# A Hyena/S5 diffusion step on one core: one taller, wider product in the filter stage, and the point-wise work of the long convolutions on VectorE alone

## The chip, the cores and the metric

The kernel runs on 1 core of one Trainium2 chip. The metric is the device time of one execution in microseconds (us). The engines are TensorE (PE; its weight loads are shown as PEld), VectorE (DVE), ScalarE (ACT), GpSimd (POOL) and SyncE (SP, which issues most transfers).

## The reference, cut to what matters

Two groups of tokens (1,024 latent, 256 context) run through a Hyena layer, an S5 layer and a feed-forward block behind each. The change lies in the Hyena layer: in the making of its filters and in its two long convolutions.

```python
def _hyena_filter_spectrum(L, w1, b1, w2, b2, w3, freq):
    ...
    h = jnp.sin(fr * (z @ w1.astype(f32) + b1.astype(f32)))
    h = jnp.sin(fr * (h @ w2.astype(f32) + b2.astype(f32)))
    h = (h @ w3.astype(f32)).reshape(L, HY_ORDER, 2, D_MODEL)
    ...
    h = h * decay[:, None, None, :]
    h = h / (jnp.sum(jnp.abs(h), axis=(0, 2), keepdims=True) + EPS)
    ...
    return jnp.fft.rfft(k, axis=0)

def _fft_longconv(v, k_f, bias):
    L = v.shape[1]
    vf = v.astype(jnp.float32)
    v_f = jnp.fft.rfft(vf, n=2 * L, axis=1)
    y = jnp.fft.irfft(v_f * k_f[None], n=2 * L, axis=1)[:, :L]
    return y + vf * bias.astype(jnp.float32)

def _hyena_mixer(u, j, p):
    ...
    v = _fft_longconv(v, k_f[:, 0], fb[0]) * x1.astype(jnp.float32)
    v = _fft_longconv(v, k_f[:, 1], fb[1]) * x2.astype(jnp.float32)
    ...
```

## The kernel before, in words

Stages follow one another on the one core: `filters` (the filters and their spectra, written to memory), `hyena_in` (input projection and short convolution, with the S5 tables beside it), `hyena_core` (the two long convolutions), `hyena_out`, a feed-forward block, the S5 scan, the gated projection and the second feed-forward block. The code only gives each engine's work; with `schedule_with_timeline_sim=True` a scheduler interleaves the steps, and each engine then runs its own list in that order.

**Products in three terms.** Where fp32 accuracy is wanted, both operands are split into a high and a low part in the format fp32r, and `mm3` (lines 35 to 38) issues hi·hi, hi·lo and lo·hi.

**`filters`, `gen` (line 415).** There are 8 units: 4 blocks `db` of 256 channels times 2 orders `o`. For each unit `gen` runs over 5 pairs `pr` of 128-row time tiles, with both directions `d` (forward and backward) of the filter. `w3s` holds the high part of the weights in partitions 0 to 63 and their low part in partitions 64 to 127. `h2h` holds the high part of the 64 hidden values twice, so one product over 128 partitions gives hi·(hi+lo) (line 424). `h2l` holds the low part once, in 64 partitions; the second product (line 425) contracts those 64 with the high part of the weights alone. Each direction has 256 columns and its own pair of products, so a time tile takes four matmuls, by turns over 128 and over 64 partitions. The DVE multiplies the result by the decay (line 426). POOL then adds and subtracts the directions (`sd`, lines 463 and 464) and sums absolute values (line 437), ACT and DVE split the result (line 467), PE transforms it (`odd`, `even`, `ctxs`), DVE combines (lines 512 to 517) and SP stores the spectrum. Beside it run the modulation products (`ada_stream`, lines 270 and 280) and the reading of x (`x_stream`).

**`hyena_core`.** 24 units: 8 groups (order, block), in each two latent halves `kt` and one context unit. `fwd` (line 753) is the forward transform on PE, from which ACT writes `E`. `point` (line 776) multiplies by the spectrum `K`: 15 point-wise steps for a latent unit and 7 for a context unit, with `AB` as scratch, each over 2 to 8 planes of 256 columns. `CUT = 168` splits every step: columns 0 to 167 go to DVE, 168 to 255 to POOL, as one instruction on each (line 813). `inverse` (line 851) is the inverse transform on PE, in fp32; in the trace each of its matmuls is two records. `evac` multiplies by the gate on DVE (line 886), `split_v` splits the result (line 226) for the second convolution. `E` has 5 buffers, `AB` and `K` two each.

Of the kernel before, what the change touches and what calls it, by code (L numbers as in the profile page):

```python
# [7 lines left out]
F32 = mybir.dt.float32  # L8
F32R = mybir.dt.float32r
# [299 lines left out]

LATW, M3W, CTXW = 4096, 1024, 512  # L310
TT = 10
CUT = 168


def load_f(K, io, fp, step=LATW + CTXW):
# [22 lines left out]
def filters(K, io):  # L338

    nc, tc = K.nc, K.tc  # L340
    V, P = nc.vector, nc.gpsimd
    ADD, SUB, MUL = ALU.add, ALU.subtract, ALU.mult
    with ExitStack() as c:
# [2 lines left out]
        hp = c.enter_context(tc.tile_pool(name="fhd", bufs=1, reuse_waits="tile"))  # L346
        cp = c.enter_context(tc.tile_pool(name="fc", bufs=1, reuse_waits="tile"))
        h2h = cp.tile([128, 1280], F32R, name="h2h")
        h2l = cp.tile([64, 1280], F32R, name="h2l")
        m3 = [cp.tile([128, M3W], F32R, name=f"m3{i}") for i in range(2)]  # L350
        W3, DEC, HD, ACC, SD, FB = {}, {}, {}, {}, {}, {}

# [14 lines left out]
        with ExitStack() as c2:  # L367
# [21 lines left out]
            for lhs, rhs, M, dst, bc in ((w1, zT, 64, a1, 0), (w2, a1, 128, a2, 1)):  # L389
                o = 0  # L390
                for n in TB:
                    ps = K.psum.tile([128, 512], F32, tag="ps", name="ps")
                    nc.tensor.matmul(ps[:M, :n], lhs, rhs[:, o:o + n], start=True, stop=True)
                    d, s = dst[:, o:o + n], t[:M, o:o + n]
                    nc.scalar.activation(out=d, in_=ps[:M, :n], func=AF.Identity, scale=bf[:M, 2:3], bias=bias[:M, bc:bc + 1])
                    reduce_2pi(K, V, d, s)
                    nc.scalar.activation(out=d, in_=d, func=AF.Sin)
                    if bc:
                        nc.scalar.copy(h2h[:, o:o + n], d)
                        V.tensor_tensor(out=h2l[:, o:o + n], in0=d[0:64], in1=h2h[0:64, o:o + n].bitcast(F32), op=SUB)  # L400
                    o += n
                    for _ in range(2 * bc):
                        next(adas)
# [11 lines left out]
        def gen(u, pr):  # L415
# [3 lines left out]
            for i in range(2):  # L419
                tt = pr * 2 + i  # L420
                ps = K.psum.tile([128, 2, 256], F32, tag="ps", name="ps")
                for d in range(2):
                    q = o * 2 + d
                    nc.tensor.matmul(ps[:, d], h2h[:, tt * 128:(tt + 1) * 128], w[:, q], start=True, stop=False)
                    nc.tensor.matmul(ps[:, d], h2l[:, tt * 128:(tt + 1) * 128], w[0:64, q], start=False, stop=True)
                V.tensor_tensor(out=hd[:, i], in0=ps, in1=dec[:, i:i + 1, :].to_broadcast([128, 2, 256]), op=MUL)
            HD[u, pr] = hd
            if o and db < 3:
# [307 lines left out]
def hyena_core(K, io):  # L736
    nc, tc = K.nc, K.tc
    with ExitStack() as c:
# [6 lines left out]
        G = gp.tile([128, LATW + CTXW], F32, name="G")  # L745
        ep = c.enter_context(tc.tile_pool(name="e", bufs=5, reuse_waits="tile"))
        ADD, SUB, MUL = ALU.add, ALU.subtract, ALU.mult
        parts = [(nc.vector, slice(0, CUT)), (nc.gpsimd, slice(CUT, 256))]

        def pl(pool, tag, n):  # L750
            return pool.tile([128, n // 256, 256], F32, tag=tag, name=tag)
# [24 lines left out]
        def point(E, Kt, ctx):  # L776

            R = 2 if ctx else 4
            AB = pl(ap, "AB", 512 * R)
            v4 = lambda t: t.rearrange("p (o a) n -> p o a n", a=2)  # L780
            todo = []
            for eng, sl in parts:
                e, w, k = (t[:, :, sl] for t in (E, AB, Kt))
                er = e.rearrange("p (a r) n -> p a r n", a=2)
                x = e
                if ctx:
                    ops = [(x[:, 2:4], x[:, 2:4], x[:, 0:2], SUB)]
                else:
                    ac = er[:, :, 2:4]
                    bd = w[:, 4:8].rearrange("p (a r) n -> p a r n", a=2)  # L790
                    ops = [(bd, er[:, :, 0:2], ac, SUB),
                           (x[:, 0:2], ac[:, :, 0], ac[:, :, 1], ADD),
                           (x[:, 4:6], ac[:, :, 0], ac[:, :, 1], SUB),
                           (x[:, 2:8:5], bd[:, :, 0], bd[:, ::-1, 1], ADD),
                           (x[:, 6:2:-3], bd[:, :, 0], bd[:, ::-1, 1], SUB)]
                ops += [(v4(w), v4(x), v4(k)[:, :, ::-1, :], MUL),
                        (x, x, k, MUL),
                        (v4(x)[:, :, 0], v4(x)[:, :, 0], v4(x)[:, :, 1], SUB),
                        (v4(x)[:, :, 1], v4(w)[:, :, 0], v4(w)[:, :, 1], ADD)]
                if ctx:  # L800
                    ops += [(w[:, 0:2], x[:, 0:2], x[:, 2:4], ADD),
                            (w[:, 2:4], x[:, 0:2], x[:, 2:4], SUB)]
                else:
                    ops += [(w[:, 0:4], x[:, 0:4], x[:, 4:8], ADD),
                            (w[:, 4:8], x[:, 0:4], x[:, 4:8], SUB),
                            (x[:, 0:2], w[:, 0:2], w[:, 2:4], ADD),
                            (x[:, 4:6], w[:, 0:2], w[:, 2:4], SUB),
                            (x[:, 6:2:-3], w[:, 4:6], w[:, 7:5:-1], ADD),
                            (x[:, 2:8:5], w[:, 4:6], w[:, 7:5:-1], SUB)]
                todo.append((eng, ops))  # L810
            for eng, ops in todo:
                for out, x, y, f_ in ops:
                    eng.tensor_tensor(out=out, in0=x, in1=y, op=f_)  # L813
            return AB if ctx else E

        order = [(0, 0), (0, 1), (1, 0), (0, 2), (1, 1), (0, 3), (1, 2), (1, 3)]
# [918 lines left out]
```

## Time and profile before

| | us |
|---|---|
| time, median of 3 runs (lowest to highest) | 3817.84 (3814.34 to 3820.59) |
| the profiled execution, its own time | 3819.98 |
| its span in the trace | 3818.1 |
| PE / DVE / POOL / ACT busy | 3440.9 / 2473.1 / 1218.6 / 964.8 |

The profile cuts the span into 40 slices of some 95 us. A digit is the busy share of an engine in that slice, in tenths; the row PEclk is the TensorE clock that was granted, in tenths of full speed. A share of the whole span is an average over stages with different limits, so the stages are read apart: `filters` lies at about 20 to 490 us of the span, `hyena_in` at 470 to 875, `hyena_core` at 875 to 1,270, and everything behind it at 1,270 to 3,818. A matmul's duration holds the draining of the array, so what one matmul costs in a row of them is the distance from its start to the next start.

### The profile page before, as it was taken

How to read it: one execution, taken by the hardware profiler on the slowest of the kernel's cores; microseconds unless marked ns; L12 is line 12 of the kernel's file. 1: busy time of each engine (PE TensorE's matmuls, PEld its weight loads, DVE VectorE, ACT ScalarE, POOL GpSimd, SP SyncE). 2: the span in 40 equal slices, each digit the busy share in tenths (PEclk: the TensorE clock that was granted, in tenths of full speed). 3: DMA queues.
4: the chain of work that ended last, by engine and by line, in shares of the span. 5: the costliest groups of instructions: out<-in, count | busy, mean ns of one | idle time of the engine just before them, and what ended most of it. 6: DMA issues, size and time to landing. Idle time of an engine off the chain costs nothing.

```text
span 3818.1 us, 48757 instructions
## 1 busy us (share of the span) xinstructions
PE 3440.9 (90%) x19238; PEld 2913.7 (76%) x19238; DVE 2473.1 (65%) x3846; ACT 964.8 (25%) x1674; POOL 1218.6 (32%) x1062
## 2 busy tenths in 40 slices
PE   6999979997777799999999998556999999999997
PEld 4777758886666588888888886555887888888886
DVE  5766798768999656655566445997236445445545
ACT  3343443332121342111111113123224111111112
POOL 3555520008999533443344001662112000000002
PEclk9777889998888899999999998777999999999998
DMA  7554545345433611222212112564101111110101
GB/s 219 175 176 155 172 153 155 121 178 190 142 116 103 201 60 60 73 69 66 67 62 70 45 39 84 137 169 133 45 28 45 34 39 39 39 39 34 45 28 56
DMA packets 292444, 368.27 MB, mean 96 GB/s; under 512 B 38415, under 2 KB 230615, under 8 KB 283256
## 3 DMA queue, kind: packets, MB, share of 16 engines
q1 hardware_dynamic: 278392, 343.53, 28.0%
q10 hardware_dynamic: 11520, 11.15, 1.3%
q0 software_dynamic: 2304, 10.49, 0.8%
q8 instruction: 152, 2.49, 0.3%
q14 instruction: 76, 0.62, 0.1%
HBM read 268.49 MB, written 91.29 MB: 94 GB/s over the span
## 4 chain that ended last, share of the span: by engine, by line
PE 55%; DVE 9%; DMA 1%; issue 1%; POOL 1%; ACT 1%; ACTq 0%; SPq 0%; DVEq 0%; POOLq 0%
PE ps L36 18%; PE ps L37 18%; PE ps L38 18%; DVE Z L1382 2%; DVE Z L1383 1%; DVE E L813 1%; DVE nw L89 1%; DVE x L1492 0%; DVE h L1334 0%; DMA yr<-yv 0%; DVE x L184 0%; DVE R L1392 0%; PE ps L1230 0%; DVE R L1391 0%; DVE AB L813 0%
## 5 line engine op out<-in xcount | busy, mean ns | idle before, releaser
L36 PE MATMUL ps<-hh,hi 128*128 128x512 f32 (+1 forms) x2688 | 953.0, 358 | 19.3 <-ACT hh L225 16.1
L37 PE MATMUL ps<-hl,hi 128*128 128x512 f32 (+1 forms) x2688 | 957.9, 357 | 8.9 <-POOL hl L96 5.8
L38 PE MATMUL ps<-hh,lo 128*128 128x512 f32 (+1 forms) x2688 | 953.2, 355 | 0.0
L184 DVE SCALAR_TENSOR_TENSOR x<-ps,mod,x 128x512 f32<-128x512 f32 (+1 forms) x1056 | 629.9, 653 | 11.3 <-PE ps L38 11.3
L36 PEld LDWEIGHTS ps<-hh,hi 128*128 128x128 f32 x2688 | 507.4, 189 | 99.9 <-ACT hh L225 17.6
L37 PEld LDWEIGHTS ps<-hl,hi 128*128 128x128 f32 x2688 | 508.6, 189 | 88.6 <-POOL hl L96 11.7
L167 DVE TENSOR_TENSOR nw<-nw,ps 128x512 f32<-128x512 f32 x132 | 78.8, 597 | 766.6 <-PE ps L38 760.8
L38 PEld LDWEIGHTS ps<-hh,lo 128*128 128x128 f32 x2688 | 507.4, 189 | 73.3 <-issue 0.5
L57 POOL TENSOR_TENSOR st<-st,sq 128x512 f32<-128x512 f32 (+1 forms) x72 | 91.7, 1277 | 1179.0 <-ACT sq L56 1176.6
L37 PE MATMUL ps<-gl,hi 128*128 128x512 f32 (+1 forms) x1056 | 375.3, 355 | 0.0
L36 PE MATMUL ps<-gh,hi 128*128 128x512 f32 (+1 forms) x1056 | 373.4, 355 | 1.2 <-DVE x L184 1.2
L38 PE MATMUL ps<-gh,lo 128*128 128x512 f32 (+1 forms) x1056 | 374.2, 354 | 0.0
L32 DVE TENSOR_TENSOR lo<-raw,hi 128x1024 fp32r<-128x1024 f32 x156 | 208.0, 1335 | 96.5 <-ACT hi L31 96.4
L31 ACT CAST hi<-raw 128x1024 fp32r<-128x1024 f32 x156 | 163.3, 1049 | 350.2 <-PE ps L37 318.1
L36 PEld LDWEIGHTS ps<-gh,hi 128*128 128x128 f32 x1056 | 198.8, 188 | 32.1 <-DVE x L184 2.1
L37 PEld LDWEIGHTS ps<-gl,hi 128*128 128x128 f32 x1056 | 199.0, 188 | 29.4 <-issue 1.2
L38 PEld LDWEIGHTS ps<-gh,lo 128*128 128x128 f32 x1056 | 199.0, 188 | 28.8 <-issue 0.7
L36 PE MATMUL ps<-hh,wh 128*128 128x512 f32 (+1 forms) x576 | 210.3, 366 | 9.8 <-ACT hh L95 9.8
L37 PE MATMUL ps<-hl,wh 128*128 128x512 f32 (+1 forms) x576 | 208.9, 363 | 7.7 <-DVE hl L92 7.4
L38 PE MATMUL ps<-hh,wl 128*128 128x512 f32 (+1 forms) x576 | 207.6, 361 | 1.8 <-POOL wl L226 1.8
L170 ACT CAST gh<-nw 128x512 fp32r<-128x512 f32 x132 | 72.2, 547 | 483.7 <-DVE nw L167 483.7
L166 ACT ACTIVATE nw<-ps 128x512 f32<-128x512 f32 x132 | 69.3, 525 | 490.9 <-PE ps L38 489.9
(369 smaller groups left out, 6153.3 us busy)
## 6 DMA issues: line engine op xcount, KB each, us to landing
adaw<-in_ada_w SPq DMA_DIRECT2D x96, 512.0 KB, 5.1
raw<-in_w13p SPq DMA_DIRECT2D x88, 512.0 KB, 3.6
raw<-in_w2p SPq DMA_DIRECT2D x44, 512.0 KB, 3.5
kspec<-KO SPq DMA_DIRECT2D x16, 1024.0 KB, 4.0
K<-kspec SPq DMA_DIRECT2D x16, 1024.0 KB, 5.2
raw<-in_hy_inp SPq DMA_DIRECT2D x24, 512.0 KB, 3.5
rot<-W SPq DMA_DIRECT2D x8, 1024.0 KB, 3.9
tin<-tst SPq DMA_DIRECT2D x32, 256.0 KB, 2.5
```

The costliest lines, as they stand in the source:

```text
L31: K.nc.scalar.copy(hi, raw)
L32: K.nc.vector.tensor_tensor(out=lo, in0=raw, in1=hi.bitcast(F32), op=ALU.subtract)
L36: nc.tensor.matmul(ps, wh, xh, start=first, stop=False, **kw)
L37: nc.tensor.matmul(ps, wh, xl, start=False, stop=False, **kw)
L38: nc.tensor.matmul(ps, wl, xh, start=False, stop=last, **kw)
L57: nc.gpsimd.tensor_tensor(out=st, in0=st, in1=sq, op=ALU.add)
L89: nc.vector.scalar_tensor_tensor(out=w, in0=x, scalar=A(k, ci), in1=K.st[tb], op0=ALU.mult, op1=ALU.mult)
L166: nc.scalar.activation(out=sa, in_=ps[0], func=AF.Silu)
L167: nc.vector.tensor_tensor(out=sa, in0=sa, in1=ps[1], op=ALU.mult)
L170: nc.scalar.copy(gh, sa)
L184: K.nc.vector.scalar_tensor_tensor(out=x, in0=p, scalar=self.G(d, COND[tb]), in1=x, op0=ALU.mult, op1=ALU.add)
L1382: V.tensor_tensor_scan(out=z[0:64, ri, 2:N + 2], data0=d[0:64], data1=x[0:64], initial=0.0, op0=MUL, op1=ADD)
```

## The change

The constant `CUT` and the loop over `parts` go. `point` issues each of its steps once, over all 256 columns, on DVE; POOL has none. In `filters`, `h2l` gets 128 partitions (the low part twice), and `gen` issues two matmuls per time tile, each over 128 partitions and over both directions at once, 512 columns.

```diff
-CUT = 168
...
-        h2l = cp.tile([64, 1280], F32R, name="h2l")
+        h2l = cp.tile([128, 1280], F32R, name="h2l")
...
-                        V.tensor_tensor(out=h2l[:, o:o + n], in0=d[0:64], in1=h2h[0:64, o:o + n].bitcast(F32), op=SUB)
+                        V.tensor_tensor(out=h2l[:, o:o + n], in0=d, in1=h2h[:, o:o + n].bitcast(F32), op=SUB)
...
-                for d in range(2):
-                    q = o * 2 + d
-                    nc.tensor.matmul(ps[:, d], h2h[:, tt * 128:(tt + 1) * 128], w[:, q], start=True, stop=False)
-                    nc.tensor.matmul(ps[:, d], h2l[:, tt * 128:(tt + 1) * 128], w[0:64, q], start=False, stop=True)
+                nc.tensor.matmul(ps, h2h[:, tt * 128:(tt + 1) * 128], w[:, o * 2:o * 2 + 2], start=True, stop=False)
+                nc.tensor.matmul(ps, h2l[:, tt * 128:(tt + 1) * 128], w[:, o * 2:o * 2 + 2], start=False, stop=True)
...
-        parts = [(nc.vector, slice(0, CUT)), (nc.gpsimd, slice(CUT, 256))]
...
-            for eng, sl in parts:
-                e, w, k = (t[:, :, sl] for t in (E, AB, Kt))
-                er = e.rearrange("p (a r) n -> p a r n", a=2)
-                x = e
+            x, w, k = E, AB, Kt
+            er = x.rearrange("p (a r) n -> p a r n", a=2)
...
-            for eng, ops in todo:
-                for out, x, y, f_ in ops:
-                    eng.tensor_tensor(out=out, in0=x, in1=y, op=f_)
+            for out, p_, q_, f_ in ops:
+                nc.vector.tensor_tensor(out=out, in0=p_, in1=q_, op=f_)
```

The list `ops` is otherwise the same. Since lines go, the changed kernel's numbers are smaller: lines 421 and 422 are the products of 424 and 425, line 804 is `point`'s 813, 858 is `inverse`'s 867.

PE in `filters`, a piece of `gen` ahead of the next unit's transforms, before (`w3s` are the weights, `h2h` and `h2l` the hidden values):

```order
141 L270 MATMUL ps<-adaw,cond 32x128 x8
142 L424 MATMUL ps<-w3s,h2h 128x256
143 L425 MATMUL ps<-w3s,h2l 128x256
144 L424 MATMUL ps<-w3s,h2h 128x256
145 L425 MATMUL ps<-w3s,h2l 128x256 x2
146 L424 MATMUL ps<-w3s,h2h 128x256
```

The same piece of PE's list with the change:

```order
114 L270 MATMUL ps<-adaw,cond 32x128 x8
115 L421 MATMUL ps<-w3s,h2h 128x512
116 L422 MATMUL ps<-w3s,h2l 128x512
117 L421 MATMUL ps<-w3s,h2h 128x512
118 L422 MATMUL ps<-w3s,h2l 128x512
```

The order among the neighbours stays; there are half as many matmuls, each of 512 columns.

PE in `hyena_core`, the inverse transforms of the second group's two latent units (`acc<-E,G`, 32 matmuls in all; `ps<-v,F` are forward transforms of later units), before, where the last 16 follow further down:

```order
3815 L38 MATMUL ps<-v,F_8212 128x256
3816 L867 MATMUL acc<-E,G 128x256 x4
3817 L36 MATMUL ps<-v,F_8211 128x256
3818 L37 MATMUL ps<-v,F_8211 128x256
3819 L38 MATMUL ps<-v,F_8212 128x256
3820 L867 MATMUL acc<-E,G 128x256 x12
```

The same place with the change (`ps<-AB,G` is the context unit's inverse):

```order
3684 L38 MATMUL ps<-v,F_8052 128x256
3685 L858 MATMUL acc<-E,G 128x256 x32
3686 L858 MATMUL ps<-AB,G 128x256 x4
3687 L280 MATMUL pm<-sel,adae 128x2
3688 L270 MATMUL ps<-adaw,cond 32x128 x8
```

Before, forward transforms of later units stood between the pieces of the inverse; with the change both latent units' inverses stand in one piece, behind all of those forward transforms.

DVE in `hyena_core`, near the beginning of the stage, where the steps of the first two latent units stand by turns, before:

```order
1290 L813 TENSOR_TENSOR AB<-E,K 128x8x168
1291 L813 TENSOR_TENSOR E<-E 128x2x168 x2
1292 L813 TENSOR_TENSOR E<-E,K 128x8x168
1293 L813 TENSOR_TENSOR E<-AB 128x2x168 x2
1294 L813 TENSOR_TENSOR E<-E 128x2x168
1295 L813 TENSOR_TENSOR E<-E 128x4x168
```

The same place with the change:

```order
1285 L804 TENSOR_TENSOR AB<-E,K 128x2048
1286 L804 TENSOR_TENSOR E<-AB 128x2x256 x2
1287 L804 TENSOR_TENSOR E<-E 128x512
1288 L804 TENSOR_TENSOR E<-E,K 128x2048
1289 L804 TENSOR_TENSOR AB<-E,K 128x2048
1290 L804 TENSOR_TENSOR E<-E 128x4x256
1291 L804 TENSOR_TENSOR E<-E,K 128x2048
```

The two units still take turns; the rows now carry all 256 columns of a plane, and POOL's list has none of them any more.

## Rows read from the trace of the kernel before

**Rows 1.** The page: engines in 40 slices of the span, and memory traffic in GB/s.
```profile
PE   6999979997777799999999998556999999999997
...
DVE  5766798768999656655566445997236445445545
...
POOL 3555520008999533443344001662112000000002
PEclk9777889998888899999999998777999999999998
...
GB/s 219 175 176 155 172 153 155 121 178 190 142 116 103 201 60 60 73 69 66 67 62 70 45 39 84 137 169 133 45 28 45 34 39 39 39 39 34 45 28 56
```
**Rows 2.** Busy time by stretch: `filters` in steady state, `hyena_core`, all else.
```profile
core 0: us, PE busy (x) PEld busy (x) DVE busy (x) ACT busy (x) POOL busy (x), PEclk, DMA share, GB/s
60.00:470.00 410.00, 388.57 (x2820) 305.72 (x2819) 281.51 (x374) 164.28 (x330) 220.99 (x138) 0.82 0.54 169
875.00:1270.00 395.00, 279.10 (x1812) 246.96 (x1810) 391.98 (x350) 78.04 (x166) 377.67 (x306) 0.83 0.39 133
...
1270.00:3818.00 2548.00, 2364.55 (x12452) 2021.99 (x12452) 1443.70 (x2106) 548.75 (x900) 567.37 (x565) 0.96 0.21 66
```
**Rows 3.** The first stretch, instructions on `w3s` alone: PE, PEld, DVE, ACT.
```profile
60.00:470.00 410.00, 124.50 (x293) 70.44 (x292) 3.67 (x3) 3.16 (x3) 0.82 0.54 169
```
**Rows 4.** PE in order of time, one piece of `filters`: start, duration, instruction.
```profile
100.19 0.39 PE L424 MATMUL ps<-w3s,h2h 128*128 128x256 f32 x1
100.50 0.38 PE L425 MATMUL ps<-w3s,h2l 64*128 64x256 f32 x1
...
107.89 0.58 PE L424 MATMUL ps<-w3s,h2h 128*128 128x256 f32 x1
108.40 0.58 PE L425 MATMUL ps<-w3s,h2l 64*128 64x256 f32 x1
...
114.14 0.41 PE L37 MATMUL ps<-sl,F 128*128 128x256 f32 x1
114.35 0.41 PE L38 MATMUL ps<-sh,F 128*128 128x256 f32 x1
...
115.84 0.28 PE L37 MATMUL ps<-sl,F 128*128 128x256 f32 x1
115.96 0.28 PE L38 MATMUL ps<-sh,F 128*128 128x256 f32 x1
```
**Rows 5.** Busy time and granted clock of the four places of rows 4.
```profile
99.00:101.50 2.50, 2.50 (x24) 1.70 (x24) 1.53 (x3) 1.51 (x3) 1.58 (x2) 1.00 0.29 73
104.00:111.00 7.00, 7.00 (x15) 3.86 (x15) 5.58 (x6) 1.06 (x1) 2.43 (x2) 0.50 0.38 117
113.00:115.00 2.00, 2.00 (x12) 2.00 (x11) 0.59 (x1) 0.20 (x1) 0.54 (x1) 0.50 0.51 140
115.70:116.70 1.00, 1.00 (x11) 1.00 (x9) 0.00 (x0) 0.00 (x0) 0.00 (x0) 1.00 1.06 377
```
**Rows 6.** PE in order of time in the second feed-forward block: matmuls of 512 columns.
```profile
3100.29 0.39 PE L37 MATMUL ps<-hl,hi 128*128 128x512 f32 x1
3100.51 0.39 PE L38 MATMUL ps<-hh,lo 128*128 128x512 f32 x1
```
**Rows 7.** `hyena_core` again, the point-wise line alone: busy time of DVE and POOL.
```profile
875.00:1270.00 395.00, 344.91 (x296) 368.51 (x296) 0.83 0.39 133
```
**Rows 8.** Groups by form, 875 to 1,270 us: busy, mean ns, idle ahead.
```profile
L813 DVE TENSOR_TENSOR E<-AB 128x336 f32<-128x336 f32 x104 | 87.9, 894 | 0.5
L813 DVE TENSOR_TENSOR AB<-E 128x672 f32<-128x672 f32 x48 | 60.5, 1291 | 8.1 <-ACT E L773 7.0 <-POOL E L813 0.5
...
L813 DVE TENSOR_TENSOR E<-E,K 128x1344 f32<-128x1344 f32 x16 | 38.6, 2412 | 0.1
...
L226 DVE TENSOR_TENSOR v<-x,v 128x512 fp32r<-128x512 f32 x20 | 26.0, 1325 | 0.0
```
**Rows 9.** DVE in order of time while POOL is idle, second feed-forward block.
```profile
3054.21 0.68 DVE L171 TENSOR_TENSOR gl<-nw,gh 128x512 fp32r<-128x512 f32 x1
3054.80 1.65 DVE L184 SCALAR_TENSOR_TENSOR x<-ps,mod,x 128x256 f32<-128x256 f32 x4
3056.37 1.21 DVE L32 TENSOR_TENSOR lo<-raw,hi 128x1024 fp32r<-128x1024 f32 x1
```
**Rows 10.** DVE in order of time inside `hyena_core`.
```profile
1016.85 3.17 DVE L813 TENSOR_TENSOR AB<-E 128x672 f32<-128x672 f32 x4
1019.94 1.75 DVE L813 TENSOR_TENSOR E<-AB 128x336 f32<-128x336 f32 x4
```

More of the change, by code (lines that the diff above doesn't have):

```diff
@@ L780, in point @@
             v4 = lambda t: t.rearrange("p (o a) n -> p o a n", a=2)
-            todo = []
-            for eng, sl in parts:
-                e, w, k = (t[:, :, sl] for t in (E, AB, Kt))
-                er = e.rearrange("p (a r) n -> p a r n", a=2)
-                x = e
[L786 to L810, printed above, removed]
@@ L811, in point @@
-            for eng, ops in todo:
-                for out, x, y, f_ in ops:
-                    eng.tensor_tensor(out=out, in0=x, in1=y, op=f_)
+            x, w, k = E, AB, Kt
+            er = x.rearrange("p (a r) n -> p a r n", a=2)
+            if ctx:
+                ops = [(x[:, 2:4], x[:, 2:4], x[:, 0:2], SUB)]
+            else:
+                ac = er[:, :, 2:4]
+                bd = w[:, 4:8].rearrange("p (a r) n -> p a r n", a=2)
+                ops = [(bd, er[:, :, 0:2], ac, SUB),
+                       (x[:, 0:2], ac[:, :, 0], ac[:, :, 1], ADD),
+                       (x[:, 4:6], ac[:, :, 0], ac[:, :, 1], SUB),
+                       (x[:, 2:8:5], bd[:, :, 0], bd[:, ::-1, 1], ADD),
+                       (x[:, 6:2:-3], bd[:, :, 0], bd[:, ::-1, 1], SUB)]
@@ new lines, in point @@
+            ops += [(v4(w), v4(x), v4(k)[:, :, ::-1, :], MUL),
+                    (x, x, k, MUL),
+                    (v4(x)[:, :, 0], v4(x)[:, :, 0], v4(x)[:, :, 1], SUB),
+                    (v4(x)[:, :, 1], v4(w)[:, :, 0], v4(w)[:, :, 1], ADD)]
+            if ctx:
+                ops += [(w[:, 0:2], x[:, 0:2], x[:, 2:4], ADD),
+                        (w[:, 2:4], x[:, 0:2], x[:, 2:4], SUB)]
+            else:
+                ops += [(w[:, 0:4], x[:, 0:4], x[:, 4:8], ADD),
+                        (w[:, 4:8], x[:, 0:4], x[:, 4:8], SUB),
+                        (x[:, 0:2], w[:, 0:2], w[:, 2:4], ADD),
+                        (x[:, 4:6], w[:, 0:2], w[:, 2:4], SUB),
+                        (x[:, 6:2:-3], w[:, 4:6], w[:, 7:5:-1], ADD),
+                        (x[:, 2:8:5], w[:, 4:6], w[:, 7:5:-1], SUB)]
```

## The prediction, made before the changed kernel was run

> **What bounds the kernel now.** I read the slices first. The reader should see two stretches [rows 1]: at the left PE is near 9 while its clock stands at 7 to 8 tenths, and around the 11th to 13th slice DVE and POOL both show 9 while PE falls to 7. The first is `filters`, the second `hyena_core`, and the change touches these two alone. The stretches give their limits [rows 2]. From 60 to 470 us PE is busy 388.6 of 410 us, DVE 281.5, POOL 221.0: PE sets the pace. From 875 to 1,270 us DVE is busy 392.0 of 395 us and POOL 377.7, PE 279.1: the point-wise work sets it. Behind 1,270 us PE is busy 93% of the time; nothing there is edited, so those 2,548 us stay, as does `hyena_in`.
>
> **Term 1, the products of `gen`.** In the steady stretch they are 293 matmuls and 124.5 us of PE [rows 3], 0.425 us each. In order of time one sees why this is dear [rows 4, 5]: at a granted clock of 1.00 (2.4 GHz) an L424 is followed by its L425 after 0.31 us, at 0.50 (1.2 GHz) after 0.51 us, while matmuls of the same 256 columns in the transforms follow each other after 0.12 and 0.21 us. The transforms' matmuls all contract 128 partitions; in `gen` 128 and 64 take turns. PE is counted as busy throughout, but PEld shows only 3.86 of 7.00 us there, against 2.00 of 2.00 in the transforms [rows 5]. I read the extra 0.2 to 0.3 us as a weight load that is not hidden when the number of partitions changes. With the change every matmul contracts 128, so the loads should hide as in the transforms.
>
> The new price: 512 columns follow each other after 0.22 to 0.23 us in the feed-forward block [rows 6], where the clock is full; at half clock I take twice the 0.21 us of 256 columns, 0.43 us. The stretch will hold 147 of them (half of 293): 33 us at full clock, 63 at half. PE's work in the stretch falls from 388.6 to 388.6 − 124.5 + 33 = 297 us, or to 327 us. I lean to the first, since the half clock in rows 5 came while `gen` ran its alternating matmuls and lasted some microseconds into the transforms; without the alternation I expect less of it, but I book no gain for the other matmuls.
>
> What becomes late next is DVE: 281.5 us of work in the same stretch, beside 221 of POOL on the same tiles. Two engines with 297 and 282 us that wait for each other do not run at 297. Today PE idles 21 us of the stretch; I allow 33. So 410 us become 330: **−80 us**. The ends: no more idle than PE's own work, 297 us, −113; PE at 327 and twice today's idle, 43 us, 370, −40.
>
> The subtraction that fills `h2l` has 128 partitions instead of 64 and the same columns, three instructions on DVE ahead of the first `gen`. Even if it took twice as long, three 512-column steps of 0.68 us [rows 9] would be 2 us. It costs nothing in the sum.
>
> **Term 2, the point-wise work.** DVE and POOL run the same 296 steps [rows 7]. What the reader must see is that each slows the other. A DVE step of 336 elements takes 894 ns in the mean, one of 672 takes 1,291 and one of 1,344 takes 2,412 [rows 8]. Four undisturbed ones of 336 took 1.75 us, 0.44 each, four of 672 took 3.17 us, 0.79 each [rows 10]. With POOL idle, 512 elements take 0.68 us and the next instruction starts 0.59 to 0.60 after it; 1,024 take 1.21 us, so 1.13 to the next [rows 9]. That is about 1.04 ns an element and 0.07 us a step; 2,048 elements, which no row shows, come to 2.20 us.
>
> On whole planes a latent unit has eight steps of 512 elements, five of 1,024 and two of 2,048: 8 × 0.60 + 5 × 1.13 + 2 × 2.20 = 14.85 us. A context unit has five of 512 and two of 1,024: 5.26 us. Sixteen and eight of them are 280 us, against 344.9 us of DVE today [rows 7]: −65 us, although DVE then does half as much again. The 20 steps of `split_v` are disturbed by POOL as well, 1,325 ns each, 26.0 us in all [rows 8]; undisturbed they cost 0.60, 12 us: −14. DVE's 392 us become 313, **−79 us**, if DVE still never waits.
>
> It will wait a little. PE's list now holds the inverses of both latent units in one piece behind the forward transforms, and DVE does the two units by turns, so PE sits until both are done, and then works at whatever clock is granted. Its busy time today, 279 us at 0.83 of the clock, is 34 us under the new 313, so PE can absorb it, but hardly twice over. I allow 12 us for the eight groups: **−67 us**. The ends: no new wait, −79; the inverses (64 records a group; at half clock 0.43 us each is 27 us, at full half of that) exposed by 5.5 us a group, −35.
>
> POOL's queue loses 296 instructions and keeps no wait for them. Behind them stand the S5 matrices' steps, which wait for memory that `hyena_core` gives back; they cannot move far forward. The spectrum and gate transfers are issued by SP in the same order, and the two stretches move 169 and 133 GB/s [rows 2]; at 330 and 328 us that is 210 and 160, which the slices show or nearly show elsewhere (219 and 201) [rows 1], so I book nothing.
>
> **The sum.** Against the profiled execution's own time, 3,819.98 us: −80 − 67 = −147, 3,673. That execution is 2.1 us above the median of the runs shown, so I predict **3671 us** for the median.
>
> **A rule that speaks against term 1.** The Trainium skill, "TensorE: Matmul & The Clock Gate", section "LDWEIGHTS (loading the stationary operand)", says that a weight load's time goes by its columns and that a load of 32 rows takes as long as one of 128. By that rule the number of partitions is no reason for a price, and the edit would only trade four matmuls of 256 columns for two of 512. The rows do not show a longer load, but an exposed one, so rule and rows need not collide; how the new ones queue, no row shows.
>
> **The rivals.**
> *The turns of 128 and 64 are not the reason.* What stays dear is `gen`'s own operands; the trade is then four matmuls for two at the price per column of the transforms, 4 × 0.12 − 2 × 0.227 = 0.026 us for each of some 74 tiles, 2 us. Against it: 0.31 and 0.51 stand right beside 0.12 and 0.21 in the same stage and clock [rows 4, 5]. For it: the loads are new for every matmul there too. Time: 3,817.8 − 2 − 67 = 3,749. Chance 0.10. The Trainium skill's rule above leads here.
> *PE becomes the bound of `hyena_core`.* With both inverses in one piece, PE starts them after a wait, at half clock, and DVE then waits for the forward transforms. If 47 more us come back, the term is −20: 3,718. For it: the clock of 0.83 in that stretch; against it: PE gains on DVE whenever it runs at full clock. Chance 0.15.
> *Both at their far ends.* PE's clock stays up in `filters` and no wait takes the place of the old: −113 − 79, 3,626. Chance 0.12.
> *Slower.* The long DVE steps are long by themselves (planes with reversed and skipping strides) and not because of POOL. Then DVE's 344.9 us grow with the elements, by 256/168, to 525.6, and the core by 181 us; with term 1 the result is 3,817.8 − 80 + 181 = 3,919. It decides the sign from about 0.92 us a step of 512 elements on: then the 280 us are 427, and the 82 us more than today's 345 eat term 1 and the gain in `split_v`, less the 12 us of waits. Against it: rows 10 show the same line at 0.44 and 0.79 us inside the stage. Chance 0.03.
>
> **How the numbers follow.** The forecast has 0.60, with its own range 3,640 to 3,705. A measurement of this kernel can tell about 0.2%, 8 us, from no change. All cases but the slower one are faster by more; faster 0.96, same 0.01, slower 0.03. The range runs from 3,615 (the far ends, and some clock regained) to 3,740 (the near ends, −40 and −35, are 3,743); it leaves out the rival at 3,749, the slower one and little else.
>
> **What would show it.** Right: L421 and L422 follow each other after 0.22 to 0.24 us, `w3s` takes 35 to 65 us of PE, `filters` ends about 80 us sooner, with DVE the busiest there; line 804 at 680, 1,215 and about 2,280 ns a step, some 280 us, and no POOL beside it; 1,270 us comes 140 to 150 sooner and everything behind takes its 2,548 us. Wrong: the new matmuls at 0.31 us or more; long DVE steps with POOL idle; PE at 0.5 clock with DVE waiting in the core; or a longer tail.

## The result, and the profile after

The changed kernel takes **3671.9 us** (median of 4 runs, 3671.1 to 3675.6), the kernel before 3816.1 (3813.8 to 3820.6) beside it. The ratio is 0.9623, with a 95% interval of 0.9606 to 0.9639. The forecast was 3,671.

Where did the 144 us come from? The first matmul of each stage on PE, in order of time, gives the stages' lengths in us (all three are of line 36: `ps<-hh,wh` begins `hyena_in`, `ps<-v,F` begins `hyena_core`, `ps<-hh,hi` begins `hyena_out`). What the prediction called the tail is here all that follows the first matmul of `hyena_out`.

| | `filters`, from 0 | `hyena_in` | `hyena_core` | the tail | span |
|---|---|---|---|---|---|
| before | 463.2 | 402.8 | 412.0 | 2,540.1 | 3,818.1 |
| after | 387.4 | 403.1 | 338.6 | 2,544.0 | 3,673.1 |
| difference | −75.8 | +0.3 | −73.4 | +3.9 | −145.0 |

The two edited stages give the whole difference, about half each. The page of the kernel after, engines in 40 slices, as [rows 1]:
```profile
PE   5889699998878999999999995549999999999997
...
DVE  5988998769995556655554548994255545455446
...
POOL 3677400000013334444331004840120000000002
PEclk8999899999988999999999997779999999999999
...
```
The reader should see three things. At the left PE has fallen from 9 to 8 and DVE has risen to 8 and 9. Where DVE and POOL both stood at 9, in the 11th to 13th slice before, DVE now stands at 9 alone, in the 10th to 12th, and POOL shows 0, 0 and 1 there. Behind that the digits are much like those of before. By stretch, columns as in [rows 2] (busy time and count of PE, PEld, DVE, ACT, POOL, then granted clock, DMA share, GB/s):
```profile
60.00:390.00 330.00, 286.07 (x2635) 245.96 (x2627) 286.63 (x372) 159.75 (x328) 221.36 (x136) 0.91 0.68 209
785.00:1120.00 335.00, 268.98 (x1908) 240.06 (x1907) 323.44 (x364) 83.24 (x175) 19.55 (x16) 0.91 0.50 170
```
`filters` has the DVE and POOL work that it had, in 330 us instead of 410, and PE's work has fallen from 388.6 to 286.1. In `hyena_core` DVE is busy 323 of 335 us, and still sets the pace. The instructions on `w3s` alone in the first stretch, to hold against [rows 3]:
```profile
60.00:390.00 330.00, 44.03 (x140) 27.39 (x140) 3.67 (x3) 3.19 (x3) 0.91 0.68 209
```
And PE in order of time (start, duration, instruction), a place where the granted clock is 1.00 and one where it is 0.50:
```profile
136.68 0.40 PE L422 MATMUL ps<-w3s,h2l 128*128 128x512 f32 x1
136.92 0.40 PE L421 MATMUL ps<-w3s,h2h 128*128 128x512 f32 x1
137.15 0.40 PE L422 MATMUL ps<-w3s,h2l 128*128 128x512 f32 x1
...
177.65 0.63 PE L422 MATMUL ps<-w3s,h2l 128*128 128x512 f32 x1
178.08 0.63 PE L421 MATMUL ps<-w3s,h2h 128*128 128x512 f32 x1
```
From start to start it is 0.23 to 0.24 us at full clock and 0.43 at half, the two prices of the forecast. Now the point-wise line, groups by form in 785 to 1,125 us of after (columns as in [rows 8]):
```profile
L804 DVE TENSOR_TENSOR E<-AB 128x512 f32<-128x512 f32 x104 | 68.3, 726 | 0.1
L804 DVE TENSOR_TENSOR AB<-E 128x1024 f32<-128x1024 f32 x48 | 57.7, 1237 | 7.5 <-ACT E L769 7.3 <-PE ps L869 0.2
L804 DVE TENSOR_TENSOR AB<-E,K 128x2048 f32<-128x2048 f32 x16 | 36.8, 2299 | 0.1
```
A step of 512 elements now takes 726 ns where one of 336 took 894 [rows 8]; one of 1,024 takes less than the 672 did. The last column matters as much: DVE waits ahead of these steps for some 8 us in all. Who waits for whom in that stage, from the table of waits (engine and line, what it waited for: us, times, longest):
```profile
PE acc L869 <- DVE E L804: 40.6, 8, 11.5
```
PE's long wait is for DVE; DVE's own waits are short.

### The profile page after: what moved, and what is told of

It reads as the page before. It is cut to its first block, busy times and chain, and to the rows that moved or that the text cites. A ratio compares the mean times of both kernels' runs of the same rounds, so it can differ in the third digit from the quotient of the medians.

```text
span 3673.1 us, 48061 instructions
## 1 busy us (share of the span) xinstructions
PE 3320.2 (90%) x19078; PEld 2840.1 (77%) x19078; DVE 2406.5 (66%) x3846; ACT 959.9 (26%) x1674; POOL 858.7 (23%) x766
## 4 chain that ended last, share of the span: by engine, by line
PE 68%; DVE 21%; DMA 5%; issue 3%; POOL 2%; ACT 1%; ACTq 0%; SPq 0%; DVEq 0%; POOLq 0%
PE ps L36 22%; PE ps L37 21%; PE ps L38 21%; DVE E L804 4%; DVE AB L804 3%; DMA adaw<-in_ada_w 1%; DVE Z L1373 1%; DVE Z L1374 1%; DMA xc<-in_xT 1%; DVE nw L89 1%; DVE sl L226 1%; DMA yr<-yv 1%; PE acc L869 1%; DVE x L89 1%; POOL h L1323 1%
## 5 line engine op out<-in xcount | busy, mean ns | idle before, releaser
L170 ACT CAST gh<-nw 128x512 fp32r<-128x512 f32 x132 | 72.3, 548 | 484.0 <-DVE nw L167 484.0
```

The source lines that it names most:

```text
L170: nc.scalar.copy(gh, sa)
```

## The experiments

All of them are timed beside the kernel before. The stages' lengths, as in the table above, are the better measure: the tail, which no edit of this study touches, lies between 2,530 and 2,544 us in the fourteen profiles, so a difference of ten us between two versions can't be put down to an edit by their totals alone.

| run | time | ratio to before (95%) | `filters` | core | tail |
|---|---|---|---|---|---|
| e1_products | 3741.9 | 0.9793 (0.9778–0.9807) | 384.2 | 413.5 | 2,536.2 |
| e2_points | 3742.3 | 0.9792 (0.9776–0.9808) | 465.4 | 339.7 | 2,532.9 |
| e3_tall_narrow | 3659.6 | 0.9579 (0.9564–0.9593) | 386.3 | 341.1 | 2,529.7 |
| e4_short_wide | 3679.6 | 0.9628 (0.9613–0.9642) | 393.0 | 341.1 | 2,534.0 |
| e5_pool_reads | 3831.3 | 1.0038 (1.0023–1.0053) | 386.4 | 500.0 | 2,537.0 |
| e6_pool_writes | 3665.7 | 0.9603 (0.9587–0.9619) | 386.2 | 336.1 | 2,540.2 |
| e13_pool_one | 3751.8 | 0.9834 (0.9819–0.9848) | 386.2 | 421.7 | 2,537.9 |
| e7_cut232 | 3689.5 | 0.9667 (0.9652–0.9681) | 388.7 | 362.5 | 2,535.2 |
| e9_sdhalf | 3678.6 | 0.9637 (0.9622–0.9651) | 396.8 | 338.5 | 2,538.8 |
| e8_ada48 | 3691.9 | 0.9681 (0.9665–0.9697) | 387.2 | 355.5 | 2,541.5 |
| e12_sd_dve | 3662.1 | 0.9594 (0.9580–0.9608) | 378.5 | 340.2 | 2,538.6 |
| e14_both | 3649.8 | 0.9557 (0.9544–0.9570) | 373.8 | 341.0 | 2,534.4 |

**One part at a time: e1_products, e2_points.** The first is the kernel before with this alone:
```
-        h2l = cp.tile([64, 1280], F32R, name="h2l")
+        h2l = cp.tile([128, 1280], F32R, name="h2l")
...
-                for d in range(2):
-                    q = o * 2 + d
-                    nc.tensor.matmul(ps[:, d], h2h[...], w[:, q], start=True, stop=False)
-                    nc.tensor.matmul(ps[:, d], h2l[...], w[0:64, q], start=False, stop=True)
+                nc.tensor.matmul(ps, h2h[...], w[:, o * 2:o * 2 + 2], start=True, stop=False)
+                nc.tensor.matmul(ps, h2l[...], w[:, o * 2:o * 2 + 2], start=False, stop=True)
```


> The kernel before with the first part of the change alone: two matmuls of 512 columns over 128 partitions in gen, while the point-wise work stays split between VectorE and GpSimd. My theory (the turns of 128 and 64 partitions leave the weight loads in the open): w3s falls from 124.5 to 35-65 us of PE, filters ends 70-85 us sooner, the rest is unchanged, the time is 3,735-3,745. Rival (the turns are not the reason, only the number of matmuls changes): w3s stays near 120 us of PE and the time is 3,810-3,816. If the gain of after in filters were really owed to the other part (VectorE's order, memory that comes free earlier), the time would also stay above 3,790.

The second has the other half of the diff: no `CUT`, no `parts`, one list of steps on `nc.vector`.

> The kernel before with the second part alone: the point-wise steps whole on VectorE, gen as before. My theory (VectorE and GpSimd slow each other, so that the split costs more than it takes off): filters ends where it did, the core between the first point and the first row of hyena_out is 67-79 us shorter, the time is 3,738-3,750. Rival (the core's gain in after came from products that ended sooner, with transfers in the core that then had more room): 3,780 or more. The two parts touch stretches that follow each other, so e1's and this one's gains should add to after's 144 within 10 us.

Alone, the products shorten `filters` by 79.0 us and leave the core at 413.5 against 412.0. Alone, the points shorten the core by 72.3 and leave `filters` 2.2 longer. The instructions on `w3s` in e1, 60 to 390 us, read as after's:
```profile
60.00:390.00 330.00, 41.86 (x140) 25.48 (x140) 3.67 (x3) 3.19 (x3) 0.93 0.69 210
```
So each part works in its own stage and needs nothing of the other. The totals fall by 77.3 and 76.9 us, 154 together against after's 144: the ten that are over lie in the tails, shorter than before's by 4 and 7 us in these two and longer by 4 in after.

**Height or number: e3_tall_narrow, e4_short_wide.** The change makes the matmuls equally tall and half as many. Each of these undoes one of the two in the changed kernel.
```
-                nc.tensor.matmul(ps, h2h[...], w[:, o * 2:o * 2 + 2], start=True, stop=False)
-                nc.tensor.matmul(ps, h2l[...], w[:, o * 2:o * 2 + 2], start=False, stop=True)
+                for d in range(2):
+                    q = o * 2 + d
+                    nc.tensor.matmul(ps[:, d], h2h[...], w[:, q], start=True, stop=False)
+                    nc.tensor.matmul(ps[:, d], h2l[...], w[:, q], start=False, stop=True)
```


> The changed kernel, but gen has its four matmuls of 256 columns again, now all of them over 128 partitions. It tells the number of partitions from the number of matmuls. My theory (height): they follow each other after 0.12 us at a granted clock of 1.00 and 0.21 at 0.50, as in the transforms; PE's w3s stays at 40-70 us, and the time is after's, 3,665-3,685. Rival (four small matmuls with operands of their own are dear by number): they stand at 0.3 and 0.5 us as before, w3s near 120 us, and most of the filters' gain is gone: 3,735-3,750.

And e4:
```
-        h2l = cp.tile([128, 1280], F32R, name="h2l")
+        h2l = cp.tile([64, 1280], F32R, name="h2l")
...
-                nc.tensor.matmul(ps, h2l[...], w[:, o * 2:o * 2 + 2], start=False, stop=True)
+                nc.tensor.matmul(ps, h2l[...], w[0:64, o * 2:o * 2 + 2], start=False, stop=True)
```


> The changed kernel, but h2l has 64 partitions again, so gen has two matmuls of 512 columns, by turns over 128 and 64. My theory (height): the weight load stays in the open at every turn, the 0.19 to 0.30 us of rows 4 on top of the 0.22 to 0.43 of the columns, so w3s goes to 65-105 us of PE and the time to 3,685-3,725, between after and the kernel before. Rival (number): two matmuls do as well over 64 as over 128, w3s as in after, 3,668-3,676.

PE in order of time at a granted clock of 1.00, first of e3:
```profile
219.20 0.28 PE L424 MATMUL ps<-w3s,h2l 128*128 128x256 f32 x1
219.32 0.28 PE L423 MATMUL ps<-w3s,h2h 128*128 128x256 f32 x1
```
and of e4:
```profile
136.35 0.50 PE L422 MATMUL ps<-w3s,h2l 64*128 64x512 f32 x1
136.78 0.50 PE L421 MATMUL ps<-w3s,h2h 128*128 128x512 f32 x1
137.21 0.49 PE L422 MATMUL ps<-w3s,h2l 64*128 64x512 f32 x1
```
This tells height from number. The same operands in the same number as before, but all over 128 partitions, follow each other after 0.12 us instead of 0.31. Half as many, but by turns of 128 and 64, stand at 0.43 instead of 0.23. Either way the turn costs 0.19 to 0.20 us at this clock, whatever the width, and in both directions. The neighbours pay as well: in the trace of before, at a granted clock of 1.00, a transform's matmul behind an L425 starts 0.31 us after it. No run has a matmul over 64 partitions behind another one, so whether short matmuls among themselves would pay is open. The weight loads themselves, in a view of e4 by tile (ns, lowest/median/highest), are equally long over 128 and 64, and as long as the price of a turn:
```profile
L421 PEld LDWEIGHTS ps<-w3s,h2h x70: 186/187/288, 82.3 to 341.2; 128*128 128x128 f32 x70
L422 PEld LDWEIGHTS ps<-w3s,h2l x70: 182/183/285, 82.7 to 341.6; 64*128 64x128 f32 x70
```
The load does not get longer, it stops being hidden. The loads in order of time show it, first one of e4, then one of after:
```profile
136.78 0.19 PEld L421 LDWEIGHTS ps<-w3s,h2h 128*128 128x128 f32 x1 [0.25 <-DVE hd L423]
```
```profile
136.69 0.19 PEld L421 LDWEIGHTS ps<-w3s,h2h 128*128 128x128 f32 x1
```
In e4 the load starts at 136.78 us together with its own matmul's row, with PEld idle before it. In after it starts 0.23 us ahead of its matmul (136.92), beside the matmul before.

The time of e4, though, is under what my theory expected. `w3s` takes 62.4 us of PE there (I had 65 to 105), 18.4 more than after (and the granted clock of the stretch is 0.96 against 0.91), and `filters` is only 5.6 us longer: PE no longer sets its pace. And e3 came out 12 us below after, 5 below the range that I gave it; the 12 us are not in `filters` (1.1 shorter), and 14 us lie in the tail. "Both directions in one matmul" brought nothing that can be seen in its stage; the 128 rows brought it all.

**Contention or waiting for halves: e5, e6, e13.** In the changed kernel GpSimd gets scratch work beside each point-wise step, which nothing reads or waits for (`dm` is a scratch tile):
```
...
                 nc.vector.tensor_tensor(out=out, in0=p_, in1=q_, op=f_)
+                n = 88 * (math.prod(out.shape) // (128 * 256))
+                nc.gpsimd.tensor_tensor(out=dm[:, 2, :n], in0=dm[:, 0, :n], in1=dm[:, 1, :n], op=ADD)
```


> The changed kernel with extra work that nothing uses: beside each of VectorE's 296 whole-plane steps GpSimd adds two scratch tiles of its own, 88 columns of each step's 256, as many as it had before the change. No data passes between the engines. It tells contention from waiting for halves. My theory (the two engines slow each other by reading and writing SBUF at the same time): line 804's 512-element steps go from 0.68 us to 0.9 or more, the core grows by 40-110 us, the time is 3,710-3,780. Rival (before, the loss was the wait for the slower half and not the neighbour): the steps stay within 5% of 0.68, 1.22 and 2.29 us, and the time is 3,665-3,680. The Trainium skill, "SBUF — State Buffer", has a lock between these two engines' reads as its rule; by that page the first.

In e6 the added line is `nc.gpsimd.memset(dm[:, 0:2, :n], 0.0)`.

> As the run with GpSimd's scratch additions, but GpSimd only fills scratch with zeros, two tiles of the same 88 columns a step: it writes SBUF and reads nothing. If the contention is over reads, VectorE's steps stay within 10% of after's and the time is 3,668-3,690. If writes count as much, the steps stretch as with the additions, and the time goes above 3,700.

In e13 it is `nc.gpsimd.tensor_scalar(out=dm[:, 2, :n], in0=dm[:, 0, :n], scalar1=1.0, scalar2=None, op0=ADD)`.

> As the run with GpSimd's scratch additions, but each extra step reads one tile (it adds a constant) instead of two, with the same columns written. It tells whether the price goes with the fact that GpSimd reads, or with its second input. If any read contends: VectorE's steps of line 804 take 0.35 us more for each microsecond that GpSimd is busy, and the time is 3,720-3,800 by how long GpSimd takes. If only two inputs on both sides contend: as after and as the run with zeros, 3,665-3,680.

Groups by form in the core, first of e5, where L807 is the point-wise line and L808 the scratch work:
```profile
L808 POOL TENSOR_TENSOR dm<-dm 128x176 f32<-128x176 f32 x165 | 195.6, 1186 | 12.9
...
L807 DVE TENSOR_TENSOR E<-AB 128x512 f32<-128x512 f32 x104 | 116.9, 1176 | 0.1
```
of e6 (L806 the points, L807 the zeros):
```profile
L806 DVE TENSOR_TENSOR E<-AB 128x512 f32<-128x512 f32 x104 | 66.6, 694 | 0.1
L807 POOL MEMSET dm<- 128x704 f32 x94 | 64.4, 685 | 5.4
```
and of e13 (L807, L808):
```profile
L808 POOL TENSOR_SCALAR dm<-dm 128x176 f32<-128x176 f32 x168 | 166.8, 993 | 13.3
...
L807 DVE TENSOR_TENSOR E<-AB 128x512 f32<-128x512 f32 x104 | 81.1, 832 | 0.1
```
The same DVE step, with the same data, takes 0.73 us with POOL idle, 0.69 beside a POOL that only writes, 0.83 beside one that reads one tile, 1.18 beside one that reads two. DVE's busy time on its 296 steps, in 785 to 1,300 us, of after, e6, e13 and e5:
```profile
785.00:1300.00 515.00, 289.09 (x296) 0.93 0.45 151
```
```profile
785.00:1300.00 515.00, 288.88 (x296) 0.94 0.45 153
```
```profile
785.00:1300.00 515.00, 333.00 (x296) 0.86 0.43 147
```
```profile
785.00:1300.00 515.00, 432.32 (x296) 0.80 0.34 117
```
Per microsecond of POOL (171.1 us in e6, 387.3 in e13, 414.6 in e5) the loss is 0, 0.11 and 0.35. The kernel before agrees with the last: after's 289 us, taken as 0.07 us a step and the rest by columns, make 197 us for 168 columns of 256, DVE took 344.9 [rows 7], 148 more for 368.5 us of POOL, 0.40. So it was contention, and it goes by what GpSimd reads.

The traces show the price more sharply step by step. DVE in order of time, first in after, then in e5 (start, duration, instruction):
```profile
832.02 1.23 DVE L804 TENSOR_TENSOR E<-E,K 128x1024 f32<-128x1024 f32 x1
833.15 1.23 DVE L804 TENSOR_TENSOR AB<-E 128x1024 f32<-128x1024 f32 x1
...
840.30 0.70 DVE L877 TENSOR_TENSOR x<-acc,x 128x512 f32<-128x512 f32 x1
840.90 2.30 DVE L804 TENSOR_TENSOR AB<-E,K 128x2048 f32<-128x2048 f32 x1
843.10 1.30 DVE L877 TENSOR_TENSOR x<-acc,x 128x512 f32<-128x512 f32 x2
```
```profile
829.93 2.64 DVE L807 TENSOR_TENSOR E<-E,K 128x2048 f32<-128x2048 f32 x1
832.50 1.57 DVE L807 TENSOR_TENSOR E<-AB 128x1024 f32<-128x1024 f32 x1
833.99 1.94 DVE L807 TENSOR_TENSOR E<-E 128x1024 f32<-128x1024 f32 x1
```
From start to start, 2,048 elements take 2.20 us in after and 2.57 in e5, 1,024 take 1.13 and 1.49. In each of the two e5 steps one GpSimd step of 176 elements ends. Sorted in this way, by the GpSimd step that ends inside, VectorE's steps have these medians from start to next start (us):

| GpSimd step | VectorE 512 elements | 1,024 | 2,048 |
|---|---|---|---|
| none (e5) | 0.60 | 1.13 | 2.20 |
| fill of 704 elements (e6) | 0.60 | 1.13 | – |
| one input, 176 elements (e13) | 0.73 | 1.27 | 2.33 |
| two inputs, 176 elements (e5) | 0.96 | 1.50 | 2.56 |
| two inputs, 352 elements (e5) | 1.33 | 1.86 | – |

A GpSimd step with two inputs of 176 elements costs 0.36 us, one of 352 costs 0.73, whatever the length of VectorE's step: 2.1 ns for each element that GpSimd works on. VectorE's own price is 1.04 ns an element (1.13 to 2.20 us for 1,024 more). While VectorE is busy, an element handed over thus costs it about twice what the element itself would.

Three of my expectations were off: e6 came out 2 us under its range; e5 cost 161 us of core, not 40 to 110, which makes it slower than the kernel before; and one input is not priced as two. Half of e13's 83 us is not VectorE's loss. DVE's last point comes 43 us later than after's, but POOL ends 45 us behind DVE, and the next stage waits for POOL's queue, as a wait of e13 shows:
```profile
ACT hh L225 <- POOL dm L808: 31.7, 1, 31.7
```
The Trainium skill, "SBUF — State Buffer", section "SBUF: two separate sides", says that VectorE and GpSimd share a port pair, and that a VectorE instruction with two SBUF inputs contends only with a GpSimd instruction that reads SBUF. The three runs agree with that: e6 costs nothing, e13 and e5 do. It also calls the lock exclusive for a whole instruction, the loser being blocked. The table fits that for VectorE, which loses a fixed time for each GpSimd step; that GpSimd is held in its turn shows in e7.

**A smaller share for GpSimd: e7_cut232.** The changed kernel with `CUT = 232` and the two lists of before.

> The changed products, with the point-wise work split again, but at column 232 of 256: GpSimd gets 24 columns where it had 88. Its 296 steps are short, and VectorE's elements fall by 24/256, which is 26 us of the 280 if nothing else changes. My theory (what GpSimd takes off is less than what its reading costs VectorE; GpSimd would be busy some 0.45 times its 368 us, and VectorE loses a share of that): the core is 10-50 us longer than after's, 3,680-3,720. Rival (a small share is nearly free, the split was only badly placed): the core is 15-25 us shorter, 3,645-3,660.

The core is 23.9 us longer than after's. The line's busy time on DVE and POOL:
```profile
790.00:1150.00 360.00, 296.40 (x296) 285.18 (x296) 0.89 0.47 156
```
VectorE has 9% fewer elements and is busy 7 us longer. 24 of 256 columns cost GpSimd 285 us, far over the 166 that I had scaled from its 368. A view of the line by tiles (ns, lowest/median/highest) shows why:
```profile
L811 POOL TENSOR_TENSOR E<-AB x120: 278/681/2242, 804.6 to 1123.9; 128x48 f32<-128x48 f32 x104, 128x96 f32<-128x96 f32 x16
```
Where VectorE is idle, a step of 48 elements takes GpSimd 0.28 us, the lowest; beside VectorE's steps it takes 0.81 in the mean. So most of that time is waiting beside VectorE, and the two engines hold each other up in turn. Both cuts that were run lose, at 168 by 73 us and at 232 by 24: the rival that a small share is nearly free is out.

**What sets `filters` now: e9_sdhalf, e8_ada48, e12_sd_dve.** In after, the waits of 60 to 390 us begin with these:
```profile
POOL sd L460 <- DVE sl L226: 59.7, 23, 5.5
ACT sh L225 <- POOL sd L461: 39.3, 14, 5.8
```
In e9 the one buffer `sd` becomes two halves:
```
-            s = hp.tile([128, 2, 2, 256], F32, tag="sd", name="sd")
...
-            split(K, s, sh, sl)
+            for j, op in enumerate((ADD, SUB)):
+                s = hp.tile([128, 2, 256], F32, tag=f"sd{j}", name="sd")
+                P.tensor_tensor(out=s, in0=hd[:, :, 0, :], in1=hd[:, :, 1, :], op=op)
+                split(K, s, sh[:, j], sl[:, j])
```


> The changed kernel, with sd's one buffer of 1,024 columns made two of 512, one for the sums and one for the differences; ScalarE's copy and VectorE's subtraction for each then have 512 columns. After the change TensorE no longer sets the pace of filters (two matmuls over 128 and 64 by turns cost it 18 us more and the stage ended only 6 us later), and GpSimd waits 59.7 us there for VectorE to give the one sd buffer back, ScalarE 39.3 us for GpSimd. My theory (the round trip through sd is what filters waits for now): that wait halves, filters ends 10-30 us sooner, the time is 3,640-3,662. Rival (it is VectorE's own load, 287 us of 330, or TensorE's): the extra instructions (40 more on VectorE at 0.07 us of fixed cost, 40 on ScalarE) change nothing or cost 3 to 6 us, 3,665-3,680.

The waits of e9, where L463 is the line of sums and differences:
```profile
POOL sd L463 <- DVE nrm L455: 47.8, 7, 8.3
...
POOL sd L463 <- DVE sl L226: 24.5, 18, 3.3
...
POOL sd L463 <- DVE hd L423: 18.7, 6, 3.6
```
The wait that I aimed at fell from 59.7 to 24.5 us, and POOL then waits for other lines of VectorE: 91 us in all. `filters` is 9.4 us longer, so my theory fell; the time lies in the rival's range, though the loss is over its 3 to 6 us. The longest wait was a symptom: as it shrank, POOL waited for VectorE at other lines.

In e8, `ADA_CORE = 48`, with a second `next(adas, None)` in each step of the core.

> The changed kernel, with 48 of the modulation columns (the matmuls of line 270 and their loads of adaw) made in hyena_core where 24 were, two a step instead of one; filters is rid of 24 and has nothing added. In hyena_core VectorE now sets the pace (323 of 335 us), TensorE 269. My theory after the runs so far (filters is set by VectorE's own list and its waits for ScalarE, TensorE and the loads each only in places): TensorE's work in filters falls by some 15-20 us, but the stage ends only 3-12 us sooner, the core stays within 5 us, and the time is 3,655-3,672. Rival (TensorE with its waits still sets filters): 15-20 us sooner, 3,645-3,657. If the columns are not free in the core: 3,675-3,690.

PE's work in 60 to 390 us falls from 286.1 to 265.3 us, and `filters` is 0.2 us shorter, where my theory had 3 to 12. In the core the moved columns are not free, and the time passes even my last case by 2 us: the stage is 16.9 us longer, PE waits for their loads, and ScalarE, which hands VectorE its input, waits for PE 90.4 us instead of 55.5:
```profile
ACT E L769 <- PE ps L38: 90.4, 73, 7.7
...
PE ps L270 <- DMA adaw<-in_ada_w: 35.8, 14, 12.5
```
With e4 (PE +19, the stage +6) and e8 (PE −21, the stage 0), TensorE by itself is out as the bound of `filters`. In e12 the change's second idea is carried over:
```
-            P.tensor_tensor(out=s[:, 0], in0=hd[:, :, 0, :], in1=hd[:, :, 1, :], op=ADD)
-            P.tensor_tensor(out=s[:, 1], in0=hd[:, :, 0, :], in1=hd[:, :, 1, :], op=SUB)
+            V.tensor_tensor(out=s[:, 0], in0=hd[:, :, 0, :], in1=hd[:, :, 1, :], op=ADD)
+            V.tensor_tensor(out=s[:, 1], in0=hd[:, :, 0, :], in1=hd[:, :, 1, :], op=SUB)
```


> The changed kernel, with the sums and differences of sd (lines 460, 461) on VectorE instead of GpSimd: the second part of the change carried over to filters. GpSimd loses 114 us there, VectorE gains 80 steps of 512 columns at 0.60 us, 48 us on top of 287. From the run with scratch additions, a microsecond of GpSimd's additions costs VectorE 0.35 us (432.3 against 289.1 us of VectorE for 414.6 us of GpSimd), so 114 us less would give back some 40. My theory: VectorE's busy time comes out within 15 us of before, the round trip through sd gets shorter, and filters ends between 10 us sooner and 10 us later: 3,662-3,682. Rival (in filters the engines overlap too little for the price to be the core's): VectorE is near 325 us busy and the stage 20-35 us longer, 3,690-3,707.

`filters` is 8.9 us shorter, the time at the near edge of my theory. Busy time to the end of the stage, first after, then e12:
```profile
60.00:387.00 327.00, 285.18 (x2632) 245.58 (x2625) 283.63 (x371) 158.15 (x325) 218.36 (x134) 0.91 0.69 211
```
```profile
60.00:378.00 318.00, 282.34 (x2633) 243.78 (x2625) 298.75 (x447) 161.03 (x321) 114.40 (x56) 0.92 0.68 213
```
VectorE has 15 us more to do and idles 19 us instead of 43. So VectorE's list alone doesn't set the stage either: its waits for the round trip through GpSimd count too. No run took work from VectorE in this stage, so how much each is worth stays open. The sums and differences themselves came out dearer than my 0.60 us, but the subtraction that follows them got cheaper, 1,313 ns from 1,601 (groups by line, e12):
```profile
L226 DVE TENSOR_TENSOR sl<-sd,sh 128x1024 fp32r<-128x1024 f32 x40 | 52.5, 1313 | 0.4 <-ACT sh L225 0.4
...
L460 DVE TENSOR_TENSOR sd<-hd 128x512 f32<-128x512 f32 x39 | 41.5, 1064 | 0.4
...
L461 DVE TENSOR_TENSOR sd<-hd 128x512 f32<-128x512 f32 x39 | 35.2, 903 | 0.0
```
**The best version: e14_both**, e12's edit and e3's together.

> The changed kernel with the two edits of the runs that came out below it: four matmuls of 256 columns in gen, all over 128 partitions, and sd's sums and differences on VectorE. My theory: the narrow matmuls are neither better nor worse than the wide ones where TensorE doesn't set the pace, and the 14 us by which that run's end was shorter behind hyena_core were not the edit's; so filters ends as with VectorE's sd alone, near 378 us, the stretch behind the core lies anywhere between the 2,530 and 2,544 us of the runs so far, and the time is 3,648-3,666. Rival (the four narrow matmuls are worth 12 us of their own): 3,644-3,654, with the shorter end again.

It takes 3649.8 us, 22 under the changed kernel, and its interval lies clear of after's. The edit of `sd` accounts for 9 of them, in `filters`. What the narrow matmuls bring, the two expectations don't settle: the total is 12 us under e12's, as e3's was 12 under after's, yet in e3 the gain stood in the tail and here it is 4.7 us in `filters` and 4.2 in the tail (the profiled execution of e14, at 3654.9, is 5 us above its median). I leave that open.

## Why the prediction was right

**Term 1, −80, was −75.8.** The cause is shown (e3, e4) and so is the price: 44.0 us of PE on `w3s`, inside the 33 to 63. Two allowances were off and cancelled. I booked no gain for the other matmuls, but the granted clock of the stretch rose from 0.82 to 0.91, and PE's other work fell from 264.1 to 242.0 us (286.1 − 44.0). An estimate from the two traces: the clock gave some 16 of these 22 us (64 us of that work ran at the half clock before, 33 after), and the rest is neighbours that had paid a turn, 25 of them at 0.19 or 0.30 us. Against that PE idles 44 us of 330, where I allowed 33. "DVE becomes late next" was right as far as it goes: more PE work costs a third of itself and less PE work brings nothing (e4, e8). Whether VectorE's work or its waits for GpSimd weigh more there, the runs leave open (e9, e12).

**Term 2, −67, was −73.4.** The ground was right: contention, and not the wait for the slower half (e5, e6, e13). So were the prices: undisturbed steps start 0.60, 1.13 and 2.20 us after one another, as forecast (lines of after beside e5). Two sizes were off and cancelled in part. DVE's list was to lose 79 us; over the whole stage its busy time fell from 396.5 to 323.4 us, 73. The row of before, columns as in [rows 2]:
```profile
866.00:1278.00 412.00, 291.41 (x1906) 258.87 (x1904) 396.50 (x360) 83.83 (x177) 382.37 (x312) 0.84 0.41 137
```
The point-wise line gave 56 us of that and not 65: its rows are busy for 289 us where the sum had 280, since a row runs 0.1 us into its successor and a few steps still stand beside POOL's steps for the S5 matrices or before a wait. `split_v`, at 13.5 us, gave 12.5 of the 14. The 12 us of new waits, on the other side, did not come at all: DVE idles 15 us of the stage before (412.0 − 396.5) and 15 after (338.6 − 323.4).

One reading of [rows 10] was wrong. Its row of four steps of "128x672" holds two of 672 elements and two of 336: in the trace they start at 1,016.85, 1,017.98, 1,019.10 and 1,019.52 us, and POOL runs until 1,018.47. So 0.79 us is no price of an undisturbed step of 672. The sum went by rows 9 and does not use it; the 0.44 of the other row, with POOL idle, stands.

**The rivals.** "The turns of 128 and 64 are not the reason" fell with e3. The Trainium skill's rule that led there ("TensorE: Matmul & The Clock Gate", "LDWEIGHTS (loading the stationary operand)": the load's time does not depend on its rows) holds in e4, 183 ns over 64 and 187 over 128. The price comes from where the load stands and not from its length. "PE becomes the bound of `hyena_core`" fell with the waits of after. "Slower", long steps by themselves, fell with after's 0.60 us from start to start, well under its deciding point of 0.92; in e5 the steps reach such prices, 432 us in all, and there the whole gain is indeed gone. "Both far ends" did not come: in `filters` PE's 286 us no longer set the stage, and in the core DVE's list lost 73 us and not 79.

**The tail** was forecast unchanged, and moved by 3.9 us. That is within what it does between versions that do not touch it. The forecast of 3,671 lies within 1 us of the 3671.9 measured, and that closeness is luck in part: the two terms came out 4 us under and 6 us over their sizes, and the tail gave back 4.

## What to carry to other kernels

A run of small matmuls that by turns contract 128 and 64 partitions pays an open weight load at every turn, 0.19 us at full clock here: give the short operand the height of its neighbours, and don't count on merging columns. (Here it was filled with a copy of itself, which adds the product of the two low parts; zeros would leave it out.) Before work is shared between VectorE and GpSimd, subtract what GpSimd's reading takes from VectorE: here 2.1 ns for each element of a step with two fp32 inputs, twice VectorE's own price for the element, so that the stage was 73 us longer with its help than without. After an edit that frees one engine, look for the next bound by adding and taking away work of each engine; the longest wait misled here.

## What the runs showed that I had not expected

- The price of a turn of heights does not depend on the columns: 0.31 against 0.12 us with 256, 0.43 against 0.23 with 512, at full clock.
- GpSimd's cost to VectorE goes by what it reads, and is a fixed time for each of its steps, not a share of VectorE's: nothing for a fill, 0.13 us for 176 elements with one input, 0.36 us with two. Two inputs of 48 elements (e7) cost 0.09 us, 0.64 against 0.55 from start to start, 1.9 ns an element.
- Work that nothing depends on can hold up a later stage by its place in a queue: 40 us of e13's 83.
- The tail differs by up to 14 us between versions that do the same work there. Its order is not always the same, since the scheduler interleaves each version anew; but e5 and e6 run it in after's order and still take 2,537.0 and 2,540.2 us against 2,544.0. Of the 14 us between after and e3, 6 lie in the first 285 us of the tail and 8 in the stretch with the S5 scan; the rest, most of both feed-forward blocks, agrees to 0.1 us. No run tells why.
